# Bias rows of a chunk-band attention: 16 DRAM-to-DRAM copies instead of four copies from SBUF rows

## The chip, the cores and the metric

The program runs on one core of a Trainium2 chip. A core has a matrix engine (PE, with its weight loads listed as PEld), a vector engine (DVE), an activation engine (ACT), a general engine (POOL) and a queue engine (SP). Here SP issues every transfer of the program; 16 DMA engines carry them out. On-chip data lie in SBUF (128 partitions) and PSUM, everything else in DRAM. The metric is the time of one execution on the device in microseconds (us); smaller is better. Differences within 0.5% are taken as no change.

## The reference

One step of a two-layer streaming encoder with 1024 prompt frames and a sample of 64 frames, width 1024, float32. Layer 0 mixes by an RWKV-7 recurrence (8 heads) and gated linear attention (GLA, 4 heads); layer 1 by softmax attention in which a frame reads its own chunk of 64 frames and the eight chunks before it, with 16 heads and a learned bias per head. Each layer ends in a SwiGLU channel mixer with hidden width 2816. What matters for the change is the bias:

```python
def rel_bias_lookup(table, rel):          # table [16, 257]
    idx = jnp.clip(rel, -128, 128) + 128
    return table[:, idx]

bias = rel_bias_lookup(rel_table, 512 + i[:, None] - j[None, :])   # i: frame of the chunk, j: key of the band
s = einsum('bhqd,bhkd->bhqk', qc, kc) * scale + bias
p = softmax(s)
```

The bias depends only on the distance between query and key, so the row of one query is the row of the query before it, moved by one place.

## The kernel before

The tokens are worked in two halves. Half A has 384 prompt frames and the 64 sample frames (448 columns), half B the other 640 frames. Activations lie transposed, features in the partitions. Every float32 operand is split into two float32r parts, so that each product takes three matmuls (L121 to L123 with the weight tile stationary, L131, L132 and L134 with the tokens stationary).

The program has four phases. The second, on which the change bears, runs from about 480 to 1240 us: the output projection of half A, then its first channel mixer (`ffn`, a generator with 22 steps, one for each tile of 128 hidden features), and beside them the RWKV-7 and GLA recurrences of half B. The third phase holds the attention of half A, the fourth that of half B; these read the bias.

*What sets the order.* The code is written with a tile framework that simulates a timeline and from it decides where each instruction stands in the list of its engine. Each engine then runs its list strictly in order. So the place of a statement in the source is only a first wish. SP's list holds all transfers; an instruction there waits for the buffers it needs, and no later transfer is issued before it. Every transfer also takes one of eight completion counters in turn (named DMAHW0 to DMAHW7), and must wait until the transfer that held this counter before has landed.

*Weights.* `load_w` (L95) fetches a weight tile of 512 KB into one of two buffers `wr`; ACT makes the high part (L98), DVE or POOL the low part (L103, L105). Four split tiles can stand ready.

*The recurrences.* Several short transfers through DRAM stand in each chunk's chain: `rkv` (L418), `xg` (L421), `rsb` (L425), `l_d` and `lt` (L531, L533), `s_d`, `t_d`, `tt` and `t` (L547 to L553) for RWKV-7, `gqkl`, `gv` and `gsg` (L696, L699, L702) for GLA; results go out by `yg_d` (L645, L751).

*The bias.* `bias_setup` runs once, in step 6 of the first channel mixer. It loads the table into 16 partitions of a tile `r` (L933), fills 127 columns with the clipped value (L934), and then writes 128 copies of each head's row of 384 floats to the DRAM scratch `bias_d` [16, 128, 384], with four transfers (L937). Each takes four rows of `r`, that is four SBUF partitions, each with 128 repeats:

```python
for q in range(4):
    nc.sync.dma_start(self.bias_d[4 * q : 4 * q + 4],
                      r[4 * q : 4 * q + 4].unsqueeze(1).to_broadcast([4, 128, 384]))
```

The attention later loads a [128, 256] tile of a head from it with a pitch of 383 (L1083), so that every partition gets the row moved by one place more.

Of the kernel before, what the change touches and what calls it, by code (L numbers as in the profile page):

```python
# [18 lines left out]
PA = 384  # prompt tokens of half A, which also holds the sample  # L19
NA, NB = PA + 64, 1024 - PA  # L20
NM = max(NA, NB)
SMP = PA  # first sample column of half A
# [6 lines left out]
MST = 128 * 128 + 128  # pitch of a matrix in scratch: one step more of its diagonal blocks  # L29
SST = 8 * (16 * 64 + 16)  # pitch of a pair of [64, 64] matrices in scratch  # L30
# columns of the vector constants
# [51 lines left out]
class Kern:  # L83
    def __init__(self, ctx, tc, a):
        self.ctx, self.tc, self.nc, self.a = ctx, tc, tc.nc, a
        self.V, self.A, self.G, self.T = self.nc.vector, self.nc.scalar, self.nc.gpsimd, self.nc.tensor
        self.wcount = 0
        self.both = False  # both vector engines on each weight tile

    # ---------------------------------------------------------------- weights  # L90
    def load_w(self, src, shape):
        """A weight tile [128, a, b] with a * b <= 1024, split in two exact float32r parts."""
        nc = self.nc
        raw = self.wp.tile(shape, F32, tag="wr", name="wr", bufs=2)
        nc.sync.dma_start(raw, src)  # L95
        hi = self.wp.tile(shape, F32R, tag="wh", name="wh", bufs=self.WB)
        lo = self.wp.tile(shape, F32R, tag="wl", name="wl", bufs=self.WB)
        self.A.copy(hi, raw)  # L98
        self.wcount += 1
        m = shape[1]  # L100
        h = m * 5 // 8 if self.both else m * (self.wcount % 2)
        if h:
            self.V.tensor_tensor(lo[:, :h], raw[:, :h], hi[:, :h].bitcast(F32), op=ALU.subtract)  # L103
        if h < m:
            self.G.tensor_tensor(lo[:, h:], raw[:, h:], hi[:, h:].bitcast(F32), op=ALU.subtract)  # L105
        return hi, lo

    def split(self, hi, lo, src):
        """hi + lo = src exactly; src an fp32 SBUF or PSUM AP."""
        self.A.copy(hi, src)  # L110
        self.V.tensor_tensor(lo, src, hi.bitcast(F32), op=ALU.subtract)

    def gemm_ws(self, w, xt, segs):
        """Weight stationary: out[seg] = w^T x^T, w [128, 8, M]; segs: list of (psum AP, first column, columns)."""
# [10 lines left out]
    def gemm_ts(self, ps, ws, hi, lo, kts, cols):  # L125
        """Token stationary: ps [tokens, 512] = sum over kts; ws: list of (whi, wlo) APs [128, 512] per kt.
        lo None: hi holds both parts."""
# [11 lines left out]
    def banks(self, hf):  # L139
        """Segments of a feature-major product over a half's tokens."""  # L140
# [4 lines left out]
    # ---------------------------------------------------------------- setup  # L145
    def setup(self):
# [31 lines left out]
        self.bias_d = d("bias_d", [16, 128, 384])  # L178
        self.base = (0, NA)
# [7 lines left out]
    def xt_tiles_in(self, pool, m):  # L187
        """Tiles of half B in place of half A's, the first m row tiles beside them."""
# [10 lines left out]
    def load_xt(self, hf, src=None, kts=range(8), cols=None, pool=None):  # L199
        """Row tiles of x^T of a half in exact parts; src: scratch or None for the input."""  # L200
# [8 lines left out]
    # ---------------------------------------------------------------- mixer constants  # L209
# [45 lines left out]
    # ---------------------------------------------------------------- input projection  # L255
    def shift_evac(self, hf, ct, segs, pool):
        """Token shift: xs = (1 - mu) p + mu p_prev."""
# [59 lines left out]
    def rs8(self, hf, ss, pool):  # L317
        """1 / sqrt(sum of squares + 1e-12) per head, with a Newton step."""
# [11 lines left out]
    def inproj_gla(self, hf, pool):  # L330
        nc, V, A, G, T = self.nc, self.V, self.A, self.G, self.T
        n, c0, xt = self.N[hf], self.base[hf], self.xt[hf]
        # decay lora: both parts of the narrow weight side by side in one stationary operand
# [56 lines left out]
    # ---------------------------------------------------------------- RWKV-7 scan  # L390
# [7 lines left out]
    def bdx(self, eng, dst, src, m):  # L398
        """dst [128, m, 2, 64] = src [128, m, 64] on the diagonal blocks, zero beside them."""
# [3 lines left out]
    def rw1(self, sp, p, n, g0):  # L403
        """Chunk quantities of one pair of heads, n chunks from scratch column g0."""
# [58 lines left out]
    def rw1b(self, sp, u):  # L463
        """Products within the chunks, and what the recurrence needs of them."""
# [5 lines left out]
        # per chunk: A_ab^T, A_rb^T, A_ak^T, A_rk^T with rows (head, s)  # L470
# [9 lines left out]
        # of each head: [alpha | rho] over [A_ak^T | A_rk^T], and A_rb^T  # L480
# [14 lines left out]
        # token-major [beta; kappa] decayed to the chunk's end; the bonus term  # L495
# [8 lines left out]
        # [state | v] and [u | v] of each chunk and head  # L504
# [8 lines left out]
    def mats(self, d, n):  # L513
        """n [128, 128] matrices in scratch, rows on partitions."""
        return bass.AP(tensor=d.tensor, offset=d.offset, ap=[[128, 128], [MST, n], [1, 128]])

    def diag16(self, d, n):
        """The 16 x 16 diagonal blocks of n [128, 128] matrices in scratch, one per row."""
        return bass.AP(tensor=d.tensor, offset=d.offset, ap=[[16 * 128 + 16, 8 * n], [128, 16], [1, 16]])

    def diag16s(self, d, n):
        """The same blocks in n pairs of [64, 64] matrices in scratch."""
        return bass.AP(tensor=d.tensor, offset=d.offset, ap=[[16 * 64 + 16, 8 * n], [64, 16], [1, 16]])

    def rw2(self, sp, u):
        """T = (I + A_ab)^-1: forward substitution in blocks of 16, then doubling; leaves T^T of each head in u.btt."""
# [17 lines left out]
        # T with rows (head, i); T^T likewise, and on the diagonal blocks  # L544
# [36 lines left out]
    def state(self, sp, p, src=None):  # L581
        """The states of a pair of heads, side by side."""
# [7 lines left out]
    def rw3(self, sp, u, S):  # L590
        """The recurrence over the unit's chunks; leaves the normalised output in u.on."""
# [26 lines left out]
        # group norm over the head dim  # L618
# [17 lines left out]
    def rw4(self, sp, u, y0):  # L636
        """y^T of a unit to scratch columns y0.. of row tile p."""
# [9 lines left out]
    def rwkv(self, hf, sp, n, src, S):  # L647
        """All units of a half, pipelined in three stages; src: initial states (None: zero). S gets the state tiles."""
# [34 lines left out]
    # ---------------------------------------------------------------- GLA  # L683
# [94 lines left out]
    # ---------------------------------------------------------------- token-major products with residual  # L778
# [12 lines left out]
    def tsg(self, hf, acc, wsrc, pairs, hi, lo, first, after=None, packed=None):  # L791
        """acc (+)= x @ W for the kt pairs given; wsrc(n, pair) -> DRAM AP of a [128, 2, 512] tile.
        packed(kt): both parts of the sample side by side.
        after(i): what follows token tile i, which makes the token tiles the outer loop."""
# [36 lines left out]
    def pack(self, pool):  # L831
        """Both parts of the sample's columns of x^T side by side."""
# [6 lines left out]
    def proj(self, hf, acc, wname, after, pool=None):  # L839
        """acc = alpha * acc + xt^T W with a [1024, 1024] weight."""  # L840
# [5 lines left out]
    def layer_norm(self, hf, acc, which, layer, out=None, transpose=True):  # L846
        """A function that normalises token tile i, to its columns of xt and to out."""
# [39 lines left out]
    # ---------------------------------------------------------------- SwiGLU  # L887
    GROUPS = (4, 8, 12, 16, 18, 22)

    def ffn(self, hf, layer, acc, hp, after):  # L890
        """acc = alpha * acc + SwiGLU(x); a step per hidden tile; after(): makes what follows each token tile."""
# [3 lines left out]
        for j in range(NHT):  # L895
# [12 lines left out]
            # half A: both parts of the sample side by side after the prompt's first part  # L908
# [18 lines left out]
    # ---------------------------------------------------------------- attention  # L927
    def bias_setup(self, pool):
        """Bias rows to scratch."""
        nc = self.nc  # L930
        r = pool.tile([128, NA], F32, tag="ht", name="r", bufs=2)[0:16, 0:384]
        # r[m] = table at relative distance 255 - m, clipped to 128
        nc.sync.dma_start(r[:, 127:384], self.a["rel_flip"])  # L933
        self.V.tensor_copy(r[:, 0:127], r[:, 127:128].to_broadcast([16, 127]))  # L934
        # 128 copies of each head's row: bias[i, 384 + j] = r[255 - (i + 128 - j)] is then a pitch of one less
        for q in range(4):
            nc.sync.dma_start(self.bias_d[4 * q : 4 * q + 4], r[4 * q : 4 * q + 4].unsqueeze(1).to_broadcast([4, 128, 384]))  # L937

    def cache_setup(self, pool):
        """Cache keys and values to scratch."""  # L940
# [20 lines left out]
    def kcols(self, hf):  # L961
        """(first half column, columns, first key column) of a half."""
        return [(0, PA, 0), (SMP, 64, 1152)] if hf == 0 else [(0, NB, PA)]

    def qk(self, hf, hp, pool, bufs):
        """Queries and keys of a pair of heads, in exact parts, to scratch."""
# [40 lines left out]
    def vproj(self, hf, pool, bufs):  # L1007
        """Values to scratch."""
# [34 lines left out]
    def attention(self, hf, hp, sp, parts=None):  # L1043
        """A pair of heads; its output, transposed, to xt of half A or to scratch of half B.
        parts: turns of space for the transposed probabilities, or None for tiles of sp."""
# [6 lines left out]
        # of each head: both parts of its values  # L1052
# [10 lines left out]
        # query tiles with their key tiles: (first column, queries, [(key tile, first key column, keys)])  # L1063
# [5 lines left out]
        for h in range(2):  # L1069
# [18 lines left out]
            for grp in groups:  # L1088
# [44 lines left out]
                # both parts of V side by side: rows of each part in one half of the product  # L1133
# [24 lines left out]
    # ---------------------------------------------------------------- all  # L1158
    def run(self):
# [11 lines left out]
        # phase 1: projections, GLA and recurrences of half A  # L1171
# [29 lines left out]
        # phase 2: output projection, channel mixer and q, k, v of half A, recurrences of half B beside  # L1201
# [22 lines left out]
        for j in self.ffn(0, 0, acc0, hp, lambda: self.layer_norm(0, acc0, "ln2", 0, xd(0))):  # L1224
            if j == 6:
                self.bias_setup(hp)
            if j == 8:
# [9 lines left out]
        # phase 3: attention of half A beside the channel mixer of half B  # L1237
# [29 lines left out]
        # phase 4: attention of half B beside the channel mixer of half A  # L1267
# [38 lines left out]
def layout(inputs):  # L1306
    """Input arrays as the kernel reads them: slices, transposes and tilings only."""
# [6 lines left out]
    def ws(w):  # [1024, M] -> [M / 128, 128, 8, 128]  # L1314
        return w.reshape(8, 128, -1, 128).transpose(2, 1, 0, 3)

    def ts(w):  # [K, 512 * J] -> [J, K / 256, 128, 2, 512]
# [56 lines left out]
```

## Time and profile before

| what | value |
|---|---|
| median of 3 runs | 3219.5 us (3208.03 to 3225.99) |
| profiled execution, its span | 3210.3 us |
| PE busy | 3047.2 us, 95% of the span |
| PEld / DVE / ACT / POOL busy | 84% / 59% / 38% / 38% |
| mean granted PE clock | 0.966 |
| bytes moved by DMA | 395.07 MB, mean 123 GB/s |
| shares of the chain that ended last | PE 80%, DVE 7%, DMA 5%, SPq 3% |

The profile is of one execution. The page gives no time for that execution outside its span, so the span is what sums are made against; it lies within the range of the timed runs, 9.2 us (0.3%) below their median. In the page's picture of the span each digit stands for one fortieth, 80.3 us, and gives the busy tenths of an engine, or the tenths of full clock that PE was granted. "SPq" in the chain of waits is time in which SP was busy with issuing a transfer. The timeline of SP lists each issue with its start and the time that the issue took, not the time of the transfer. In the table by windows each row has the window, its length, the busy time of each engine with the number of its instructions, the granted PE clock, the mean busy share of the 16 DMA engines and the bytes that they moved per second.

### The profile page before, as it was taken

The page shows a single profiled execution, that of the slowest core. Times are in us where ns is not written, and L with a number is a line of the kernel's source. Part 1 is how long each engine was busy: PE and PEld are TensorE (multiplying, and loading weights), DVE is VectorE, ACT ScalarE, POOL GpSimd, SP SyncE. Part 2 cuts the span into 40 slices and gives each one's busy share as a digit, 9 for nine tenths or more (in the row PEclk, how much of TensorE's full clock was granted, in tenths as well). Part 3 has the DMA queues.
Part 4 walks back from the last instruction along what each step waited for, and adds up shares of the span by engine and source line. Part 5 has one row for each costly group of instructions (what it writes and reads, how often), then busy time and mean ns, then how long its engine had stood idle before and what let it go on. Part 6 is the DMA issues. An engine that isn't in the chain of part 4 may idle for free.

```text
span 3210.3 us, 50190 instructions
## 1 busy us (share of the span) xinstructions
PE 3047.2 (95%) x17732; PEld 2712.3 (84%) x17732; DVE 1899.3 (59%) x4786; ACT 1208.4 (38%) x2657; POOL 1222.4 (38%) x1373
## 2 busy tenths in 40 slices
PE   8999998998189999999999999999999999999998
PEld 7888887787078887888899989899999997999997
DVE  5677875977089866455555364544666667533335
ACT  4554554344044432424443222345444442222211
POOL 2354533544045433434333232334545444322223
PEclk9989998799589999999999999999999999999999
DMA  6543445433233324834333232676444543322221
GB/s 204 142 152 115 110 119 130 126 96 97 41 106 105 106 88 156 262 115 133 119 119 97 98 102 73 205 207 195 141 146 128 145 141 113 115 79 79 75 77 66
DMA packets 297066, 395.07 MB, mean 123 GB/s; under 512 B 125120, under 2 KB 218152, under 8 KB 296816
## 3 DMA queue, kind: packets, MB, share of 16 engines
q1 hardware_dynamic: 296816, 391.88, 40.4%
q8 instruction: 140, 2.29, 0.3%
q14 instruction: 110, 0.90, 0.1%
HBM read 316.29 MB, written 75.49 MB: 122 GB/s over the span
## 4 chain that ended last, share of the span: by engine, by line
PE 80%; DVE 7%; DMA 5%; SPq 3%; issue 2%; ACT 1%; POOL 1%; POOLq 0%; another core or an unknown queue 0%; DVEq 0%; ACTq 0%
PE gps L121 14%; PE gps L123 14%; PE gps L122 14%; PE gps L131 8%; PE gps L132 8%; PE gps L134 7%; PE op L1147 2%; PE tp L1121 2%; PE sps L1105 1%; PE sps L1106 1%; PE ps L613 1%; SPq L696 1%; SPq L937 1%; PE pb L475 1%; DVE x L542 1%
## 5 line engine op out<-in xcount | busy, mean ns | idle before, releaser
L121 PE MATMUL gps<-xh,wh 128*128 128x320 f32 (+1 forms) x2892 | 964.4, 334 | 8.4 <-ACT xh L206 5.8
L122 PE MATMUL gps<-xl,wh 128*128 128x320 f32 (+1 forms) x2892 | 963.2, 333 | 0.6 <-DVE xl L207 0.6
L123 PE MATMUL gps<-xh,wl 128*128 128x320 f32 (+1 forms) x2892 | 962.6, 333 | 1.0 <-DVE wl L103 0.7
L105 POOL TENSOR_TENSOR wl<-wr,wh 128x384 fp32r<-128x384 f32 (+2 forms) x333 | 574.9, 1731 | 907.9 <-ACT wh L98 880.8
L98 ACT CAST wh<-wr 128x1024 fp32r<-128x1024 f32 x396 | 413.5, 1048 | 713.3 <-issue 238.6
L121 PEld LDWEIGHTS gps<-xh,wh 128*128 128x128 f32 x2892 | 546.9, 189 | 30.2 <-ACT xh L206 5.8
L123 PEld LDWEIGHTS gps<-xh,wl 128*128 128x128 f32 x2892 | 546.6, 189 | 20.5 <-DVE wl L103 1.8
L122 PEld LDWEIGHTS gps<-xl,wh 128*128 128x128 f32 x2892 | 546.5, 189 | 19.0 <-DVE xl L207 1.0
L103 DVE TENSOR_TENSOR wl<-wr,wh 128x640 fp32r<-128x640 f32 (+2 forms) x333 | 318.1, 956 | 335.0 <-ACT wh L98 330.2
L131 PE MATMUL gps<-wh,hh 128*128 128x512 f32 x792 | 314.1, 398 | 0.6 <-DVE acc L815 0.6
L1116 POOL TENSOR_SCALAR s<-s,mx 128x640 f32<-128x640 f32 (+5 forms) x144 | 203.2, 1411 | 287.6 <-DVE mx L1115 249.0
L132 PE MATMUL gps<-wl,hh 128*128 128x512 f32 x792 | 312.3, 396 | 0.0
L134 PE MATMUL gps<-wh,hl 128*128 128x512 f32 x704 | 274.7, 396 | 1.6 <-DVE hl L913 1.5
L815 DVE TENSOR_TENSOR acc<-acc,gps 128x512 f32<-128x512 f32 (+1 forms) x216 | 144.9, 680 | 107.2 <-PE gps L134 101.0
L134 PE MATMUL gps<-wh,xl 128*128 128x512 f32 (+1 forms) x441 | 175.8, 403 | 5.0 <-DVE xl L207 4.8
L131 PE MATMUL gps<-wh,xh 128*128 128x512 f32 (+1 forms) x441 | 175.5, 404 | 3.6 <-DVE acc L813 3.6
L131 PEld LDWEIGHTS gps<-wh,hh 128*128 128x128 f32 x792 | 149.7, 189 | 32.8 <-DVE acc L815 3.3
L132 PE MATMUL gps<-wl,xh 128*128 128x512 f32 (+1 forms) x441 | 176.0, 401 | 1.0 <-DVE wl L103 0.8
L132 PEld LDWEIGHTS gps<-wl,hh 128*128 128x128 f32 x792 | 149.7, 189 | 28.9 <-DVE wl L103 0.2
L907 DVE SCALAR_TENSOR_TENSOR ht<-ht,gps 128x320 f32<-128x320 f32 (+1 forms) x132 | 69.6, 528 | 174.9 <-PE gps L123 174.8
L540 DVE TENSOR_TENSOR t<-lt,x 16x48 f32<-16x48 f32 (+9 forms) x540 | 148.1, 274 | 34.5 <-DMA lt<-l_d 24.6
L1114 ACT ACTIVATE s<-s,mx 128x640 f32<-128x640 f32 (+5 forms) x144 | 96.5, 670 | 176.6 <-DVE mx L1113 173.4
(288 smaller groups left out, 4949.8 us busy)
## 6 DMA issues: line engine op xcount, KB each, us to landing
wr<-in_w_fi SPq DMA_DIRECT2D x176, 512.0 KB
wr<-in_w_fo SPq DMA_DIRECT2D x88, 512.0 KB
wr<-in_w_in SPq DMA_DIRECT2D x44, 512.0 KB
wr<-in_w_qk SPq DMA_DIRECT2D x32, 512.0 KB
qs<-qd SPq DMA_DIRECT2D x32, 320.0 KB
wr<-in_w_om SPq DMA_DIRECT2D x16, 512.0 KB
wr<-in_w_v SPq DMA_DIRECT2D x16, 512.0 KB
vd<-vh SPq DMA_DIRECT2D x16, 512.0 KB
```

The costliest lines, as they stand in the source:

```text
L98: self.A.copy(hi, raw)
L103: self.V.tensor_tensor(lo[:, :h], raw[:, :h], hi[:, :h].bitcast(F32), op=ALU.subtract)
L105: self.G.tensor_tensor(lo[:, h:], raw[:, h:], hi[:, h:].bitcast(F32), op=ALU.subtract)
L121: self.T.matmul(ps, hi[:, kt, :], xh, start=(kt == 0), stop=False)
L122: self.T.matmul(ps, hi[:, kt, :], xl, start=False, stop=False)
L123: self.T.matmul(ps, lo[:, kt, :], xh, start=False, stop=(kt == nk - 1))
L131: self.T.matmul(ps, hi(kt)[:, cols], wh, start=(i == 0), stop=False)
L132: self.T.matmul(ps, hi(kt)[:, cols], wl, start=False, stop=(lo is None and i == n - 1))
L134: self.T.matmul(ps, lo(kt)[:, cols], wh, start=False, stop=(i == n - 1))
L540: V.tensor_tensor(tv, lt[:, j, w:16].unsqueeze(2).to_broadcast([m, r, w]), x[:, 0, j, 0:w].unsqueeze(1).to_broadcast([m, r, w]), op=ALU.mult)
L815: self.V.tensor_tensor(a, a, ps[:m], op=ALU.add)
L1116: G.tensor_scalar(s[:m, :nk], s[:m, :nk], mx[:m, 3:4], None, op0=ALU.mult)
```

## The change

`bias_setup` no longer writes the copies. It stores the 16 rows once to a new small DRAM scratch `brow_d` [16, 384]. A new function copies the row of one head 128 times from there, from DRAM to DRAM; it is called for two heads in each of the steps 12 to 19 of the same channel mixer.

```diff
         self.bias_d = d("bias_d", [16, 128, 384])
+        self.brow_d = d("brow_d", [16, 384])
...
     def bias_setup(self, pool):
...
         nc.sync.dma_start(r[:, 127:384], self.a["rel_flip"])
         self.V.tensor_copy(r[:, 0:127], r[:, 127:128].to_broadcast([16, 127]))
-        for q in range(4):
-            nc.sync.dma_start(self.bias_d[4 * q : 4 * q + 4], r[4 * q : 4 * q + 4].unsqueeze(1).to_broadcast([4, 128, 384]))
+        nc.sync.dma_start(self.brow_d, r)
+
+    def bias_copies(self, h):
+        self.nc.sync.dma_start(self.bias_d[h], self.brow_d[h : h + 1, :].to_broadcast([128, 384]))
...
         for j in self.ffn(0, 0, acc0, hp, lambda: self.layer_norm(0, acc0, "ln2", 0, xd(0))):
             if j == 6:
                 self.bias_setup(hp)
+            if 12 <= j < 20:
+                for h in range(2 * j - 24, 2 * j - 22):
+                    self.bias_copies(h)
             if j == 8:
```

`bias_d` and all that reads it stay as they are. In the built program the lists of the five engines hold the same work as before, apart from SP's; around this place some instructions of the recurrences and of the channel mixer, which do not depend on each other, have changed places by a few rows.

The first place is SP's list from the load of the table on. In it `bias_d<-r` is a copy of four rows (L937 before), `brow_d<-r` the store of the 16 rows (L936 now) and `bias_d<-brow_d` the copy of one head (L940 now). Before:

```order
L933 DMA r<-in_rel_flip 16x257
L95 DMA wr<-in_w_fo 128x1024
L937 DMA bias_d<-r 512x1x384 x2
L696 DMA gqkl<-qkl_d 128x3x64
L418 DMA rkv<-rkv_d 128x3x128
L937 DMA bias_d<-r 512x1x384 x2
L645 DMA yg_d<-y 128x128
L421 DMA xg<-xg_d 128x2x128
L699 DMA gv<-gv_d 64x128 x2
```

And now, where the store has the place of the first pair, and the first nine head copies follow it:

```order
L934 DMA r<-in_rel_flip 16x257
L95 DMA wr<-in_w_fo 128x1024
L936 DMA brow_d<-r 16x384
L697 DMA gqkl<-qkl_d 128x3x64
L419 DMA rkv<-rkv_d 128x3x128
L940 DMA bias_d<-brow_d 128x384 x4
L646 DMA yg_d<-y 128x128
L940 DMA bias_d<-brow_d 128x384
L422 DMA xg<-xg_d 128x2x128
L700 DMA gv<-gv_d 64x128 x2
L940 DMA bias_d<-brow_d 128x384 x4
```

The loads `gqkl` and `rkv` now stand behind one small store; the copies still stand in front of `xg` and `gv`.

The second place is SP's list right behind this, with the chain of the RWKV-7 recurrence (`s_d`, `t_d`, `lt`, `tt`, `t`) and the weights. Before:

```order
L547 DMA s_d<-x_9302 16x16x16
L548 DMA t_d<-x_9302 16x16x16
L533 DMA lt<-l_d 16x16x16
L551 DMA tt<-s_d 64x2x64 x2
L553 DMA t_9337<-t_d 128x2x128
L95 DMA wr<-in_w_fi 128x1024
L751 DMA yg_d<-gy 128x2x64
L702 DMA gsg<-sg_d 128x2x64
L95 DMA wr<-in_w_fi 128x1024
```

And now:

```order
L548 DMA s_d<-x_9303 16x16x16
L549 DMA t_d<-x_9303 16x16x16
L534 DMA lt<-l_d 16x16x16
L940 DMA bias_d<-brow_d 128x384 x2
L552 DMA tt<-s_d 64x2x64 x2
L554 DMA t_9338<-t_d 128x2x128
L95 DMA wr<-in_w_fi 128x1024
L940 DMA bias_d<-brow_d 128x384 x2
L752 DMA yg_d<-gy 128x2x64
L703 DMA gsg<-sg_d 128x2x64
L940 DMA bias_d<-brow_d 128x384 x3
L95 DMA wr<-in_w_fi 128x1024
```

The last seven copies stand between the transfers of this chunk; behind the last row shown no copy follows. The source asks for two copies in each of eight steps, while the list has all 16 in one knot, from the third row behind the store on.

The third place is the head of the knot, with what each transfer waits for (DMAHW names a completion counter):

```order
L936 DMA brow_d<-r 16x384 [waits DMAHW3_49,DVE_49]
L697 DMA gqkl<-qkl_d 128x3x64 [waits DMAHW6_49,DVE_49,Pool_49]
L419 DMA rkv<-rkv_d 128x3x128 [waits DMAHW7_49,DVE_49,PE_49]
L940 DMA bias_d<-brow_d 128x384 [waits DMAHW5_49,DMAHW0_49]
L940 DMA bias_d<-brow_d 128x384 [waits DMAHW1_49]
L940 DMA bias_d<-brow_d 128x384 [waits DMAHW2_49]
```

The first copy waits for two counters: the one that it takes over, and the one of the store of the rows that it reads. The others wait only for the counter that they take over.

## The prediction

> **What bounds the kernel now.** I read the page first, for the engine that sets the end and for a place where it does not.
>
> ```profile
> PE   8999998998189999999999999999999999999998
> PEclk9989998799589999999999999999999999999999
> PE 80%; DVE 7%; DMA 5%; SPq 3%; issue 2%; ACT 1%; POOL 1%; POOLq 0%; another core or an unknown queue 0%; DVEq 0%; ACTq 0%
> ```
>
> PE is full nearly everywhere, and the chain that ended last is PE's for 80%. One slice stands out: the eleventh (803 to 883 us) has PE at a tenth. SP's 3% of the chain is about 96 us, also unusual. So I asked for the chain around that slice.
>
> ```profile
> 790.23 27.73 SPq L696
> 821.93 10.30 SPq L937
> 832.28 17.08 SPq L937
> 849.40 23.38 SPq L645
> 885.41 2.38 DMA s_d<-x
> ```
>
> The chain here is no computation but SP issuing transfers, one of them for 27.73 us. SP's own timeline shows that this is not the usual price.
>
> ```profile
> 738.23 0.48 SPq L645 DMA_DIRECT2D yg_d<-y  x1
> 757.04 0.43 SPq L696 DMA_DIRECT2D gqkl<-qkl_d  x1
> 777.16 9.82 SPq L937 DMA_DIRECT2D bias_d<-r  x2
> 787.08 30.88 SPq L696 DMA_DIRECT2D gqkl<-qkl_d  x1
> 821.93 27.43 SPq L937 DMA_DIRECT2D bias_d<-r  x2
> 849.40 23.38 SPq L645 DMA_DIRECT2D yg_d<-y  x1
> ```
>
> An issue that took 0.43 us at 757 takes 30.88 us behind the first two bias copies, and 23.38 us in place of 0.48 behind the second pair. The copies are the cause: the queue is full of them and takes nothing until they drain. The victims are on DVE, then on PE:
>
> ```profile
> 841.43 0.29 DVE L704 TENSOR_TENSOR_SCAN gb<-m,gqkl 128x64 f32<-128x64 f32 x1 [53.57 <-DMA gqkl<-qkl_d]
> 888.09 0.28 DVE L536 COPY x<-eye 16x256 f32<-16x256 f32 x1 [40.06 <-DMA t_d<-x]
> ```
>
> DVE waits 53.57 us for `gqkl`, and everything behind it in DVE's list waits too, also the channel mixer's `hl` and `ht` that PE needs; then 40.06 us for a round trip of the recurrence. What this costs and how the copies run can be read from windows.
>
> ```profile
> 700.00:790.00 90.00, 90.00 (x572) 77.55 (x571) 79.45 (x256) 42.78 (x133) 45.23 (x80) 0.98 0.37 102
> 790.00:800.00 10.00, 4.54 (x24) 3.82 (x23) 0.00 (x0) 0.50 (x2) 0.22 (x1) 0.93 0.23 25
> 800.00:840.00 40.00, 0.00 (x0) 0.00 (x0) 0.00 (x0) 0.00 (x0) 0.00 (x0) 0.50 0.26 34
> 840.00:850.00 10.00, 5.01 (x25) 4.18 (x26) 5.89 (x20) 2.77 (x6) 0.61 (x1) 0.51 0.24 34
> 850.00:860.00 10.00, 3.26 (x15) 2.42 (x13) 0.00 (x0) 0.00 (x0) 0.00 (x0) 0.83 0.24 40
> 860.00:890.00 30.00, 0.00 (x0) 0.00 (x0) 1.15 (x5) 0.00 (x0) 0.00 (x0) 0.50 0.26 63
> 890.00:900.00 10.00, 9.00 (x33) 6.69 (x34) 7.99 (x29) 4.26 (x13) 4.59 (x7) 0.50 0.45 135
> 900.00:990.00 90.00, 90.00 (x585) 77.07 (x583) 82.37 (x279) 45.95 (x141) 47.48 (x82) 0.99 0.40 110
> ```
>
> Between 800 and 840 nothing computes at all. The DMA share is 0.26, which is four of 16 engines, and they move 34 GB/s; before and after, 102 GB/s take a share of 0.37. A copy reads four SBUF partitions and is carried by four engines.
>
> **The change part by part.**
>
> *Removed: the four copies from SBUF.* The loss is counted in matmuls. From 790 to 900 us PE did 24 + 25 + 15 + 33 = 97 instructions (two stand on a border and are counted twice). In the 90 us ahead it did 572, 6.36 each us, in the 90 us behind 585, 6.50. So 110 us held the work of 14.6 to 15.0 us. The clock says the same: 4.54 + 3.26 us near full clock and 5.01 + 9.00 us at 0.50, counted half, are 14.8. The stall cost 110 − 14.8 = **95.2 us**. On both sides of it PE is busy for 90.00 of 90.00 us, with the same recurrences beside it, so time won here is not lost again to a wait that already stands there.
>
> *Added: the store `brow_d<-r`.* It moves 24 KB. The chain has a store of that size, `s_d<-x` (16 KB), with 2.38 us. The first head copy waits for its landing, and behind it in SP's list stand `yg_d`, `xg` and `gv`. I take up to 2.4 us of SP; `gqkl` and `rkv`, which were the late ones, are now issued before that wait.
>
> *Added: 16 head copies.* They move the same 3.15 MB (16 x 128 x 384 x 4 bytes). No transfer of before goes from DRAM to DRAM, so their price is bounded by what is nearest:
>
> ```profile
> 630.27 0.35 SPq L851 DMA_DIRECT2D gb<-in_ln_w  x1
> 630.66 0.43 SPq L851 DMA_DIRECT2D gb<-in_ln_b  x1
> 632.00:634.00 2.00, 2.00 (x10) 1.29 (x9) 2.00 (x9) 0.84 (x4) 1.61 (x3) 0.50 0.85 322
> L1083 SPq DMA_DIRECT2D bias<-bias_d x32: 327/538/642, 1315.7 to 2554.4; - x32
> ```
>
> The two `gb` loads are the nearest kin on the read side: one row of DRAM (4 KB here, 1.5 KB in the change) sent to 128 places. Within 2 us of them the engines moved 322 GB/s at a share of 0.85. At that rate 3.15 MB take 9.8 us. The steady work gives 102 / 0.37 = 276 GB/s for a full share, 11.4 us. If reading and writing DRAM in one transfer halved the rate, it would be 22.8 us; if the single row throttled all engines to the 34 GB/s of the old copies, 92.5 us. I take 11.4, since the kin shows no throttling; the last case is a rival below.
>
> These 11.4 us meet other traffic. All 16 copies stand in one knot of SP's list. The other transfers among them, some 20, are about a chunk's worth, and one chunk follows the other in 19 to 20 us (`gqkl` at 737.79 and 757.04):
>
> ```profile
> 737.79 0.38 SPq L696 DMA_DIRECT2D gqkl<-qkl_d  x1
> ```
>
> In 20 us the others need 20 x 0.37 = 7.4 us of all engines. With the copies that is 18.8 of 20: busy, not overloaded. On SP the 16 issues cost 16 x 0.54 = 8.6 us (the median of L1083's issues, which also address DRAM rows); SP has room, since some 20 issues at the 0.43 to 0.54 us of the rows above are about 10 of 20 us. A group of four copies is 768 KB, 2.9 us at 276 GB/s, and delays what is queued behind it by so much.
>
> Who waits for that: behind the first groups stand `xg` and `gv`, behind the next `l_d` and `lt`, behind the pairs `tt`, `t` and the weights. Weights are asked for as soon as a buffer is free, as SP's own waits show:
>
> ```profile
> SPq L95 <- DVE wl L103: 1016.8, 226, 24.2
> ```
>
> SP waits 1016.8 us in all for the split of an older tile, not for want of time, so with four split tiles ahead 3 us don't reach PE. The chain of `l_d`, `lt`, `s_d`, `tt` does reach PE's list, which is in order. If none of the delays shows, the price is 0. If copies, issues and the landing all lie on PE's path, it is 11.4 + 8.6 + 2.4 = 22.4 us. I take **5 us**, nearer to nothing, because PE showed no idle time with this chain at its side (90.00 of 90.00), and because the scheduler put some of the recurrence's matmuls some rows later here.
>
> [...]
>
> For the sum I don't add a fixed part to each copy: eight counters let up to eight fly at once.
>
> *Unchanged.* The bias tiles are read from the same scratch with the same pattern (L1083), not before 1315.7 us, so the copies have 500 us of room, and only their company matters. DVE's fill of `r` stays.
>
> *The sum.* 3210.3 − 95.2 + 5.0 = 3120.1 us of span, 90.2 less. The profiled execution's span is 9.2 us below the runs' median; I take the difference from that median: 3219.5 − 90.2 = **3129.3 us**.
>
> **The rivals.**
>
> *A smaller stall takes the place.* The knot, at half the rate of my estimate, needs 22.8 + 7.4 = 30.2 us of DMA in 20 us; the rest pushes the recurrences' round trips ahead of it, and in-order SP holds `xg` and the weights behind waits for counters. For it: all 16 stand together, not over eight steps. Against it: the steady share of 0.37 leaves room. It becomes visible above 22 us; at 40 us of stall the time is 3219.5 − 95.2 + 40 = 3164 us.
>
> *The change doesn't do what it says.* What the copies need is not more engines but another source; if one row of DRAM is as slow as one group of SBUF rows, at 34 GB/s, the 3.15 MB take 92.5 us again, the queue is as full as before, and the result is 3219 us within a few. Against it stands the `gb` row with 322 GB/s.
>
> *Slower than before.* All 16 engines read the same 1.5 KB of DRAM, 128 times a head. If that one place serves them at a rate below the old copies', every engine is held, not four, and nothing else moves. The four old copies held the chain for about 107 us (790 to 897), so the point from which this decides is 3.15 MB / 107 us = 29 GB/s. At 25 GB/s, the lowest row above, the knot lasts 126 us, 19 more: 3219.5 + 19 + 2.4 = 3241 us. For it: a single address; against it: `gb` again, though its row is 2.7 times as long.
>
> [...]
>
> **How the numbers follow.** Forecast (stall gone, new price 0 to 22.4 us): 0.85. Smaller stall: 0.08. No gain: 0.03. Slower: 0.04. The forecast's own times run from 3219.5 − 95.2 = 3124 to 3147; the runs before lay between 11 us below and 6 us above their median, so the range goes from 3108 to 3155, which takes in the milder end of the smaller stall and leaves out about 0.15. A measurement of this kernel tells about 0.5%, 16 us, from no change. Faster: 0.85 + 0.08 = 0.93; within 0.5%: 0.03; slower: 0.04.
>
> **What would show it.** In the changed kernel's profile the page should have no slice with PE at 1; the windows of 700 to 900 us should have PE busy throughout with some 6.4 instructions each us; no issue on SP should last above a few us; in some 20 to 25 us around the copies the DMA share should rise towards 0.9 at over 200 GB/s, not stay at a quarter; the chain should hold SPq well under 1%. DVE's waits for `gqkl` and `t_d<-x` should be single microseconds. I am wrong if a window of over 22 us without PE remains near 780 us, if SP's issues of L940 take many microseconds, or if PE idles elsewhere in the second phase for what was won here.

## The result, and the profile after

The changed kernel takes 3123.4 us (median of 4 runs, 3116.2 to 3127.0); the kernel before took 3214.3 us in the 4 runs beside it. The ratio is 0.970 (0.967 to 0.973): 3.0% faster. The profiled execution has a span of 3119.8 us, 90.5 less than the 3210.3 of before; the forecast was 90.2 less, 3129.3 us for the runs. Two executions, one of the kernel before and one of an experiment, had a lower granted clock (0.87 and 0.84 in place of 0.97 to 0.98), took 3 to 6% longer and enter no ratio below.

The page of the changed kernel, the same three rows as shown of before:

```profile
PE   8999999799999999999999999999999999999998
PEclk9989999889999999999999999999999999999999
PE 83%; DVE 8%; DMA 5%; issue 2%; ACT 1%; POOL 1%; SPq 1%; POOLq 0%; DVEq 0%; ACTq 0%
```

The slice with PE at 1 is gone, and so is the one with half the clock. SPq falls from 3% of the chain to 1%, as the page rounds it. SP's timeline at the same place (start, time of the issue):

```profile
781.75 0.33 SPq L936 DMA_DIRECT2D brow_d<-r  x1
782.45 0.37 SPq L697 DMA_DIRECT2D gqkl<-qkl_d  x1
784.61 3.33 SPq L940 DMA_DIRECT2D bias_d<-brow_d  x4
788.06 0.52 SPq L646 DMA_DIRECT2D yg_d<-y  x1
806.46 1.76 SPq L940 DMA_DIRECT2D bias_d<-brow_d  x3
```

`gqkl`, which took 30.88 us to issue, takes 0.37, and `yg_d` 0.52 in place of 23.38. The whole knot of 16 copies is issued within 24 us (784.6 to 808.2). Windows of the changed kernel, with PE's busy time, its instructions, the clock, the DMA share and GB/s as before:

```profile
700.00:780.00 80.00, 78.78 (x496) 67.38 (x495) 71.13 (x228) 38.68 (x115) 39.20 (x65) 0.98 0.38 107
784.00:814.00 30.00, 28.60 (x185) 24.13 (x185) 24.93 (x83) 12.27 (x38) 13.65 (x21) 1.00 0.71 197
840.00:900.00 60.00, 60.00 (x401) 52.72 (x401) 54.30 (x175) 30.55 (x98) 33.04 (x53) 1.00 0.41 113
```

Around the copies the engines are at 0.71 and 197 GB/s, and PE loses 1.40 of 30 us. That loss is one wait, on PE's timeline:

```profile
809.82 0.50 PE L134 MATMUL gps<-wh,hl 128*128 128x512 f32 x1 [1.40 <-DVE hl L914]
```

In the chain, `hl` comes behind ACT's pieces `wh` and `hh`, and these behind ACT's copy of `t`, a transfer of the recurrence; the store `s_d<-x` ahead of that took 4.45 us, where it took 2.38 before. The wait for `hl` is PE's only one in these 30 us. One of 1.22 us on the same line stands at 703.50, long ahead of the copies, so it is not sure that the 1.40 us are theirs.

Two signs came in part only: the prediction had the DMA share near the copies rise towards 0.9 at over 200 GB/s, and SPq fall well under 1% of the chain; the rows have 0.71 at 197 and a rounded 1%.

Where the time came from can be fixed by two landmarks, the load of the table (`r`) and the second issue of `rkv` behind it, in the chunk of the recurrence that follows the copies. Before:

```profile
774.73 0.41 SPq L933 DMA_DIRECT2D r<-in_rel_flip  x1
899.94 0.36 SPq L418 DMA_DIRECT2D rkv<-rkv_d  x1
```

After:

```profile
779.22 0.41 SPq L934 DMA_DIRECT2D r<-in_rel_flip  x1
812.71 0.36 SPq L419 DMA_DIRECT2D rkv<-rkv_d  x1
```

The stretch took 125.2 us and takes 33.5, so 91.7 us were won in it. The rest of the program gave back about 1 us net: it starts 4.5 us later in this execution, and takes 3.3 us less behind the landmark (2307.1 against 2310.4). All but that 1 us of the gain stayed.

### The profile page after: what moved, and what is told of

The parts are those of the page before. It is cut to its first block, busy times and chain, and to the rows that moved or that the text cites. A ratio compares the mean times of both kernels' runs of the same rounds, so it can differ in the third digit from the quotient of the medians.

```text
span 3119.8 us, 50207 instructions
## 1 busy us (share of the span) xinstructions
PE 3038.1 (97%) x17732; PEld 2705.3 (87%) x17732; DVE 1898.4 (61%) x4786; ACT 1208.7 (39%) x2657; POOL 1228.6 (39%) x1373
## 4 chain that ended last, share of the span: by engine, by line
PE 83%; DVE 8%; DMA 5%; issue 2%; ACT 1%; POOL 1%; SPq 1%; POOLq 0%; DVEq 0%; ACTq 0%
PE gps L121 14%; PE gps L122 14%; PE gps L123 14%; PE gps L131 8%; PE gps L132 8%; PE gps L134 8%; PE op L1150 2%; PE tp L1124 2%; PE sps L1108 1%; DVE t L541 1%; DVE x L543 1%; PE sps L1109 1%; PE ps L614 1%; DVE wl L103 1%; PE pb L476 1%
```

## The experiments

The gain was as forecast, but a right number doesn't show why the old copies were slow, nor why slow copies stopped PE. The change does three things at once: another source, more engines for a copy, and smaller copies between other transfers. The theories: *source* (four neighbouring SBUF rows cannot be read faster than the 34 GB/s of before), *engines* (a copy of four rows goes to four engines, the share of 0.26), *cutting*. Each ratio below is to the kernel before on the same chip. The last column is the stretch between the two landmarks in the profiled execution.

| kernel | ratio to before (95%) | profiled span, us | stretch, us |
|---|---|---|---|
| kernel before | 1 | 3210.3 | 125.2 |
| changed kernel | 0.970 (0.967 to 0.973) | 3119.8 | 33.5 |
| DRAM, four copies, four engines | 0.979 (0.977 to 0.981) | 3146.9 | 54.9 |
| DRAM, four copies, 16 engines | 0.972 (0.968 to 0.975) | 3117.1 | 34.4 |
| SBUF, one copy of 16 rows | 0.978 (0.976 to 0.980) | 3134.9 | 52.4 |
| SBUF, 16 copies of a row | 0.998 (0.996 to 0.999) | 3202.7 | 123.1 |
| SBUF, four copies, rows four apart | 0.977 (0.974 to 0.980) | 3140.4 | 52.3 |
| half by DRAM, half old, issued by ACT | 0.987 (0.984 to 0.989) | 3170.0 | 84.2 |
| the same, issued by SP | 0.987 (0.985 to 0.990) | 3171.6 | 86.3 |
| old copies issued by POOL | 0.980 (0.977 to 0.983) | 3149.6 | 59.0 |
| no copies | 0.970 (0.966 to 0.973) | 3122.3 | 31.6 |
| 32 copies from DRAM | 0.970 (0.967 to 0.973) | 3126.8 | 35.0 |

### The source changed: four copies from DRAM

```diff
-            nc.sync.dma_start(self.bias_d[4 * q : 4 * q + 4], r[4 * q : 4 * q + 4].unsqueeze(1).to_broadcast([4, 128, 384]))
+            nc.sync.dma_start(self.bias_d[4 * q : 4 * q + 4], self.brow_d[4 * q : 4 * q + 4].unsqueeze(1).to_broadcast([4, 128, 384]))
```

(with `brow_d` stored from `r` ahead of it, as in the change. In the built order the four copies now stand together behind `gqkl` and `rkv`, so their place differs a little too.)

> The kernel before, with the 16 rows stored once to DRAM and the same four large copies made from there: outermost dimension 4, 768 KB each, all in SBUF's old place of the program. Only the source changes. Source theory (the four SBUF rows of a copy can be read at some 27 to 34 GB/s and no faster, and that filled the queue): the copies are still on four engines, but a packet of 1.5 KB should take near the 65 ns that it took in the changed kernel, not 224 ns; 512 packets on each of the four engines are 33 us, so most of the stall goes and 10 to 30 us of it stay: a span of 3125 to 3145 us. Engine theory (four engines are slow whatever they read): packets as slow as before, a drain of about 105 us, a span of about 3210 us. Cutting theory (what helped was that small copies stand between other transfers): about 3210 us.

Measured 3143.9 us, a span of 3146.9, 2 us above the expected range. A window of this kernel in the copies, with the issue of the four:

```profile
790.00:810.00 20.00, 16.05 (x95) 13.35 (x94) 9.45 (x26) 4.99 (x17) 7.25 (x9) 1.00 0.27 100
784.74 19.01 SPq L939 DMA_DIRECT2D bias_d<-brow_d  x4
```

Still four engines (a share of 0.27), but 100 GB/s in place of 34: each engine does about 23 GB/s, not 8. The median packet of 1.5 KB took 65 ns, where it took 224 in the kernel before. So four engines alone are not why the old copies were slow, and some 70% of the gain (63 of 90 us of span) come with the source, without any cutting. That the copies' new place is not the reason is shown by the kernel with rows apart, below, which keeps the old place.

### The same with the repeats outermost

```diff
+            nc.sync.dma_start(self.bias_d[4 * q : 4 * q + 4].rearrange("h i d -> i h d"),
+                              self.brow_d[4 * q : 4 * q + 4].unsqueeze(0).to_broadcast([128, 4, 384]))
```

> As the first, but each of the four DRAM copies has the 128 repeats outermost, so that all 16 engines can carry it; still four copies of 768 KB in one place. Source theory and engine theory: 3.15 MB at about 300 GB/s are 10 to 12 us, no stall worth the name, a span of 3116 to 3128 us, the same as the changed kernel. Cutting theory: the copies are neither small nor spread, so the queue is blocked as before, about 3210 us, or at the least well above the changed kernel's 3120.

Measured 3122.0 us, the median of three executions. The profile below is of one more.

> The second kernel of the first set once more, for a profile at full clock. Source and engine theory: a span of 3114 to 3128 us, over 250 GB/s in the windows of the copies, PE without a gap of over 5 us near them.

The span was 3117.1 us. The window of the copies:

```profile
784.00:798.00 14.00, 14.00 (x95) 12.08 (x93) 12.48 (x39) 6.03 (x19) 7.96 (x11) 1.00 0.94 291
```

All engines (0.94) at 291 GB/s, and PE is not touched in these 14 us. Four copies of 768 KB in one place do what 16 copies of 192 KB do. The cutting has no share in the gain that the runs can tell, nor has the spread over eight steps, which the built order did not have anyway. The 20 to 30 us that the first kernel lacked (22 by the runs, 21 by the landmarks, 30 by the spans) are the four engines: 3.15 MB at 100 GB/s are 31 us, at 291 they are 11. Of the 4.1 MB that 291 GB/s are in 14 us, 3.1 MB are rows of 1.5 KB that are read 128 times each; that they are read from so few places in DRAM is no brake here: 291 GB/s at 0.94 would be 310 for a full share, the steady work's 102 at 0.37 only 276.

### All 16 SBUF rows in one copy

```diff
-        for q in range(4):
-            nc.sync.dma_start(self.bias_d[4 * q : 4 * q + 4], r[4 * q : 4 * q + 4].unsqueeze(1).to_broadcast([4, 128, 384]))
+        nc.sync.dma_start(self.bias_d, r.unsqueeze(1).to_broadcast([16, 128, 384]))
```

> The kernel before with one copy of all 16 SBUF rows in place of four of four rows. Source theory, if a group of four neighbouring partitions is the slow unit: four groups are read at once, about 109 to 136 GB/s, 23 to 29 us for the 3.15 MB, packets of 1.5 KB again at about 224 ns since four engines still share a group; a stall of 10 to 25 us, a span of 3125 to 3140 us. Engine theory: 16 engines at full rate, 65 ns a packet, 8 to 12 us, a span of about 3120 us. Cutting theory: one copy of 3 MB is the worst case, 3210 us or more.

Measured 3141.4 us, a span of 3134.9, as the source theory had it. The window:

```profile
790.00:810.00 20.00, 6.22 (x34) 5.23 (x32) 2.75 (x11) 0.56 (x2) 2.81 (x6) 0.75 0.92 101
```

Here the share is 0.92, nearly all engines, and they move 101 GB/s, where the DRAM kernel moved 291. 16 rows are four groups of four neighbours; three times what one group gave in the kernel before (34, with the other traffic in it).

### 16 copies of one SBUF row each

```diff
+        for h in range(16):
+            nc.sync.dma_start(self.bias_d[h : h + 1], r[h : h + 1].unsqueeze(1).to_broadcast([1, 128, 384]))
```

> The kernel before with 16 copies of one SBUF row each (the 128 repeats are then the outermost dimension, so 16 engines can carry one), in the old place; the scheduler puts them between the other transfers as in the changed kernel. The cutting is that of the change, the source is the old one. Source theory: each copy reads one row at 27 to 34 GB/s with all 16 engines held in it, 92 to 117 us for all, packets of 1.5 KB far above 224 ns (towards 900); the queue is as blocked as before: a span of 3200 to 3225 us. Engine theory: 16 engines, about 12 us in all, a span of about 3120 us. Cutting theory: about 3120 us.

Measured 3207.3 us, 0.2% under the kernel before: the stall is nearly whole, 123.1 us between the landmarks. The window:

```profile
805.00:850.00 45.00, 0.00 (x0) 0.00 (x0) 0.00 (x0) 0.00 (x0) 0.00 (x0) 0.50 0.84 36
```

This is the change's cutting with the old source, 16 engines at each copy (0.84), and 36 GB/s. It settles the two: neither cutting nor engines help while the source is one row. The engines only wait longer: the median packet of 1.5 KB took 785 ns.

### Four rows, but not neighbours

```diff
-            nc.sync.dma_start(self.bias_d[4 * q : 4 * q + 4], r[4 * q : 4 * q + 4].unsqueeze(1).to_broadcast([4, 128, 384]))
+            nc.sync.dma_start(self.bias_d[q::4], r[q::4].unsqueeze(1).to_broadcast([4, 128, 384]))
```

> The kernel before with one thing changed: each of the four copies takes every fourth row of the table (rows q, q + 4, q + 8, q + 12) in place of four neighbours. The source is still SBUF, a copy still has four rows and goes to four engines. If what is slow is a group of four neighbouring partitions, read by four engines at once, each engine now has a group of its own: some 100 GB/s in the windows of the copies as in the first DRAM kernel, a drain of about 32 us, a span of 3135 to 3150 us. If any SBUF row that is read 128 times is slow, or four engines are, 27 to 40 GB/s again and a span of 3200 to 3225 us.

Measured 3140.5 us, a span of 3140.4. The window:

```profile
800.00:810.00 10.00, 5.62 (x26) 4.72 (x27) 5.90 (x20) 2.77 (x6) 0.62 (x1) 0.68 0.27 100
```

Four engines and SBUF as before, and 100 GB/s, just as with DRAM. What was slow is neither SBUF nor a repeated row as such, but that all reads of a copy went to one group of neighbouring partitions. How far apart rows must be is not measured beyond this step of four. Neighbours gave 25 to 40 GB/s for one group of four (the kernel before, windows from 790 to 860 us) and 101 for four groups in one copy, the other traffic included. How many engines a copy had went with its outermost dimension, where SP issued it: a share of 0.26 and 0.27 with four rows outermost, 0.92 with 16, and 0.94 and 0.84 with the 128 repeats outermost.

### Who holds PE: issued by another engine

Why did slow copies stop PE? My reading was that SP's own queue stood full. Then the same copies in another queue should do no harm. POOL first:

```diff
-            nc.sync.dma_start(self.bias_d[4 * q : 4 * q + 4], r[4 * q : 4 * q + 4].unsqueeze(1).to_broadcast([4, 128, 384]))
+            nc.gpsimd.dma_start(self.bias_d[4 * q : 4 * q + 4], r[4 * q : 4 * q + 4].unsqueeze(1).to_broadcast([4, 128, 384]))
```

> The kernel before with the four copies of four SBUF rows issued by POOL in place of SP: the same slow source and the same four engines, but SP's queue is not filled by them. Queue theory (PE stood because SP could issue nothing while the copies drained): the copies still take some 100 us, the other transfers pass them, and the stall shrinks to 0 to 30 us: a span of 3118 to 3145 us. Engine theory of the stall (each of the other transfers has a share on the four held engines and lands only when these have carried it): the loads are as late as before, a span of 3180 to 3215 us.

Measured 3154.3 us, between the two. A window and the time from issue to landing of the four copies:

```profile
800.00:810.00 10.00, 0.04 (x1) 0.05 (x1) 1.43 (x7) 0.07 (x1) 0.00 (x0) 0.61 1.01 109
DMA to landing us min/median/max: 35.3/39.1/40.2
```

The premise failed: from POOL's queue the copies used all engines (1.01) and ran side by side at 109 GB/s, so they were over in 40 us, not 100. The kernel is another form of the one copy of 16 rows, and can't be set against 100 us. Two pieces of its chain tell something else, though (start, time):

```profile
782.19 26.16 DMA rkv<-rkv_d
809.71 15.85 DMA s_d<-x
```

SP issued `rkv` in 0.37 us, as usual, and it landed only 26 us later; `s_d<-x` took 15.85 us, where it took 2.38 before. So transfers that SP had issued were late while the slow copies kept all engines busy.

Half of the old copies went to ACT next, with the other half from DRAM, and the same with SP as a control:

```diff
+        nc.sync.dma_start(self.brow_d, r)
+        for q in range(2):
+            nc.scalar.dma_start(self.bias_d[4 * q : 4 * q + 4], r[4 * q : 4 * q + 4].unsqueeze(1).to_broadcast([4, 128, 384]))
+        for q in range(2, 4):
+            nc.sync.dma_start(self.bias_d[4 * q : 4 * q + 4].rearrange("h i d -> i h d"),
+                              self.brow_d[4 * q : 4 * q + 4].unsqueeze(0).to_broadcast([128, 4, 384]))
```

> Two of the four old copies (heads 0 to 7) stay as they were but are issued by ACT; the other two come from DRAM with the repeats outermost. The slow copies are then 1.57 MB, on the same four engines and the same neighbouring rows, some 46 to 58 us at 27 to 34 GB/s, in another queue than SP's. Queue theory (the stall came from SP's own queue standing full): SP issues at its usual pace, ACT is held for about 10 us by its two issues; a span of 3118 to 3132 us. Engine theory (any transfer has a part on the four held engines and is late with them, whoever issued it): SP's loads are late by most of the drain, a span of 3145 to 3170 us, near that of the next kernel.

> The control of the one before: the same two old copies and the same two DRAM copies, all issued by SP. Half the slow bytes: if the stall is their drain, 40 to 55 us of it stay, a span of 3155 to 3175 us by either theory.

Measured 3171.1 and 3173.4 us, the same. About half of the stall stays for half of the slow bytes, whoever issues them, so SP's full queue as the only cause falls. But the rows name other holders beside the one that I had set against it. From the kernel with ACT, two pieces of its chain (start, time), a piece of SP's timeline, and its longest wait on a copy (in total, times, longest):

```profile
777.90 33.68 DMA bias_d<-r
811.66 0.37 SPq L422
812.07 7.24 SPq L700 DMA_DIRECT2D gv<-gv_d  x2
ACT ht L903 <- DMA bias_d<-r: 38.2, 1, 38.2
```

SP issued nothing from about 795 us (`yg_d` ends there) until the first copy, issued by ACT at 777.90, had landed at 811.6: in the built order `xg` (L422) waits for DMAHW5, that copy's completion counter, and takes it over. From 819.3 to 842.6 us it stood again, since the weight load behind `gv` takes over the counter of the second copy. And ACT waited 38.2 us for the second copy to land, because the channel mixer's `ht` takes the buffer of `r`, which the copies read; in the order it waits for the counters of both. In the control the chain of waits went another way, by an issue of 26.89 us on SP and the landing of a DRAM copy:

```profile
800.56 26.89 SPq L941 DMA_DIRECT2D bias_d<-brow_d  x2
819.65 27.01 DMA bias_d<-brow_d
```

That the two kernels end alike fits one more thing: in both the second slow copy landed at 842.6 to 842.7 us, and in both `ht`, which waits for it, ran right behind (at 842.67 and 842.79).

The engines that carry the slow copies are a holder too, the one that I had expected. The trace keeps completion marks of the transfers, 16 of `gqkl` and of `rkv`. In ACT's kernel `rkv`, issued at 779.19 us, has twelve marks at 781.3 to 782.0 and the last four at 800.4 to 800.8. In the kernel before, `gqkl` has twelve at 819.3 to 819.6 and four at 836.6, 839.5, 841.2 and 841.3, and DVE's `gb`, which waits for it, ran at 841.43. The second slow copy has its last four marks there at 836.2, 839.2, 840.9 and 841.0, each 0.3 to 0.4 us ahead of one of `gqkl`. Four of the 16 marks, as many as the engines that the slow copies took, came late.

So a slow copy held the program in four ways: the issue behind it in its own queue, the counter that it occupied, the buffer that it read, and the engines that carried it: four of the 16 marks of `gqkl` and of `rkv`, as many as these, came late. Not all are seen in each kernel: in the kernel before, ACT's `ht` ran at 846.14 us, while copies were still reading `r`, so the buffer did not hold it there. What each is worth alone is not separated; no kernel with `r` in a buffer of its own was run.

### The price of the new copies

The floor without copies:

```diff
-            bd = self.bias_d[2 * hp + h]
-            nc.sync.dma_start(bias[:, bw - 256 :], bass.AP(tensor=bd.tensor, offset=bd.offset + 127, ap=[[383, 128], [1, 256]]))
+            bd = self.brow_d[2 * hp + h]
+            nc.sync.dma_start(bias[:, bw - 256 :], bass.AP(tensor=bd.tensor, offset=bd.offset + 127, ap=[[0, 128], [1, 256]]))
```

> The rows are stored once to DRAM and no copies are made; the attention loads its bias tiles of the same size and shape from the one row, without the shift by one place for each query (so the part of the bias that moves with the query is left out). All else is the changed kernel. This is the floor under the changed kernel. My sum (16 copies cost about 5 us): from the issue of the table's load to the second issue of rkv behind it, which took 33.5 us in the changed kernel, it should take 29 to 31 us, and the span 3112 to 3120 us. Rival (the copies still hold a stall, or the freed time was given back elsewhere in the second phase because of them): a span under 3105 us.

Measured 3123.7 us, a span of 3122.3, 2 us above the expected range. The landmarks of this kernel:

```profile
776.05 0.41 SPq L934 DMA_DIRECT2D r<-in_rel_flip  x1
807.66 0.36 SPq L419 DMA_DIRECT2D rkv<-rkv_d  x1
```

31.6 us, also a little above the 29 to 31 expected, against 33.5 with the 16 copies: 1.9 us for them in this stretch, in one execution of each. PE was busy for 30.00 of the 30 us from 781 to 811. In the timed runs nothing of it is left; the two ratios are the same to a thousandth. And twice the copies:

```diff
         self.nc.sync.dma_start(self.bias_d[h], self.brow_d[h : h + 1, :].to_broadcast([128, 384]))
+        self.nc.sync.dma_start(self.bias2_d[h], self.brow_d[h : h + 1, :].to_broadcast([128, 384]))
```

> The changed kernel with each head's copy made twice, the second time into a scratch that nobody reads: 32 copies, 6.3 MB, in the same stretch. My sum (the price grows with the DMA time, some 11 us of all engines for each 16 copies, of which a third reaches PE): the same stretch takes 37 to 45 us, a span of 3123 to 3132 us. Rival of the smaller stall (beyond what the engines have free in one chunk the delay goes to PE in full): 20 us and more, a span over 3138 us. If the 16 copies cost nothing at all, 32 cost nothing either: 3120 us.

Measured 3122.9 us. The window of all 32:

```profile
785.00:840.00 55.00, 52.38 (x328) 43.19 (x327) 45.13 (x152) 22.40 (x69) 24.37 (x41) 1.00 0.76 195
```

These are 6.3 MB in all, and PE loses 2.6 of 55 us, where it lost 1.4 of 30 with 16 copies. I had expected the landmarks 37 to 45 us apart; they were 35.0 (780.20 to 815.17), since the second half of the copies came only behind them. The span of 3126.8 us lies in the expected range, but within the scatter of the runs it fits no cost as well, so this run only bounds the price: a few us for 32 copies, below what the runs can tell.

## Why the prediction was right, and where not

*The stall of 95.2 us.* Right. With the landmarks it can be taken without counting matmuls: 125.2 us before, 31.6 without copies, 93.6 us.

*The price of 5 us.* A little large: 1.9 us by the landmarks of one execution each, and none that the timed runs show. The sum was 3120.1 us of span, the measured one 3119.8. Partly that is luck: the stall was put 1.6 us too high and the price 3.1, and about 1 us was given back elsewhere, which nearly cancels. The agreement is closer than the scatter of the runs (3116 to 3127) deserves.

*The price's parts.* The nearest row was well chosen: the `gb` loads ran at 322 GB/s, and the kernel with the repeats outermost, with rows of 1.5 KB, at 291 with a share of 0.94. The halved rate and the 34 GB/s did not come. The knot's demand was put at 18.8 us of all engines within 20; measured are 0.71 of the 30 us from 784 to 814, about 21, so it was spread thinner than forecast. The 16 issues took 10.4 us of SP in SP's timeline, not 8.6.

*"The queue is full of them and takes nothing until they drain."* This step was wrong as the whole cause, though the rows it rested on are true. The issues of 20 to 30 us were the last thing in the chain, not the only thing that held: of `gqkl`, issued at last at 818 us, the last four of 16 marks came only at 836.6 to 841.3, each right behind one of a slow copy. With half of the copies in ACT's queue the stall was as long as with that half in SP's, held by two counters, a buffer and the engines. The prediction took the eight counters only as room for the new copies to fly in (in the changed kernel seven transfers were under way at 790.8 us, begun by then and their last marks still to come), and spoke of held engines only in the rival *Slower than before*. It did no harm, because the change removed the slow copies and with them all holders at once.

*"A copy reads four SBUF partitions and is carried by four engines."* True, but it left open which of the two counts, and the "not more engines but another source" of the second rival set them against each other rightly. It is the four neighbours: four engines (a share of 0.27) did 100 GB/s with rows apart, 16 engines (0.84) did 36 with one row.

*The rivals.* The smaller stall and the two cases of a slow DRAM row did not come: rows of 1.5 KB ran at 291 GB/s. That the 16 copies stand in one knot was right, and nearly without weight: even with 32 copies PE lost only 2.6 of 55 us.

*The range.* By its own working, 3124 less 11 to 3147 plus 6, it would go from 3113 to 3153; it was given as 3108 to 3155. The measured median lies in both.

*The median.* 90.2 us were taken from the 3219.5 us of the first three runs. With the fourth run the median of before is 3214.3, and 3214.3 − 90.2 = 3124.1 is within 1 us of the measured median. Most of the miss of 6 us is that of the base.

## What to carry to other kernels

For some 94 us here four slow transfers stopped a program that had much DMA time to spare (a share of 0.37 ahead of them): look in SP's timeline for issues of many us (30.88 here), and in the windows for a DMA share and a rate that don't fit each other (0.26 at 34 GB/s here, against 0.37 at 102). For copies of a few SBUF rows into many places, rows four partitions apart gave 100 GB/s here in place of 34, DRAM rows 100 with four rows outermost (a share of 0.27) and 291 with the 128 repeats outermost (0.94); whether the pieces had 192 or 768 KB made no difference (3123.4 and 3122.0 us). Moving slow copies from SP's queue to ACT's cured nothing here, since their counters (until 811.6 and 842.6 us) and their buffer (38.2 us) were waited for and the last four of 16 marks of `rkv` came 18 us behind the first twelve.

## What was not expected of the hardware

More engines on one SBUF row did not help: 16 copies of single rows kept 0.84 of all engines busy for 36 GB/s, and the stall was nearly as long as with four engines at 0.26. DRAM rows of 1.5 KB that are each read 128 times ran at 291 GB/s with a share of 0.94, where the rows of 4 KB had 322 at 0.85. Beside a slow copy on four engines the last four of 16 marks of `gqkl` and `rkv` came some 13 to 22 us behind the first twelve, whether SP or ACT had issued it. The same four-row copies issued by POOL went to all engines (1.01) and ran side by side at 109 GB/s, where from SP they went one after the other at 34.
